# A two-layer decoder trunk: token-major residual and down projections by seven products of halves

## The chip, the cores and the metric

The kernel runs on one core of a Trainium2 chip. The metric is the device time of one execution in microseconds (us); lower is better. The time before is 1746.85 us, the median of three runs (1746.84 to 1747.02).

## The reference

There are 512 tokens of 1024 channels in float32 and two layers. Each layer is

```
x = x + 1/2 * (silu(h @ w1) * (h @ w3)) @ w2      h = rmsnorm(x, g1), 2816 hidden channels
h = rmsnorm(x, gm);  p = h @ w_in                 2048 columns, eight pieces of 256
y = concat(conformer_conv, short_gated_conv, multiscale_pool, chunked_spatial_gating)
x = x + y @ w_out
x = x + 1/2 * swiglu(rmsnorm(x, g2))              as the first line, with its own weights
```

and the output is `rmsnorm(x, final_norm)`. The four mixers are causal over the tokens; the conformer part is a depthwise convolution of 31 taps with a layer norm, a sigmoid gate before it and a silu behind it. `rmsnorm` divides by the root of a token's mean square over the 1024 channels and multiplies by a gain.

## The kernel before

All activations are channel-major: a tile holds 128 channels on the partitions and the 512 tokens along the row. The residual is eight such tiles, `xt[0..7]`.

Each matrix product keeps float32 accuracy with three fast products. A float32 operand is split into a rounded part, `hi`, and a remainder, `lo`. For weights, ScalarE makes `hi` (L92, a copy with a change of type) and VectorE makes `lo = raw - hi` (L94); the same is done for activations. `mm3` (L97) then issues hi\*hi, hi\*lo and lo\*hi into one PSUM bank. Weights arrive by DMA on SyncE's queue in pieces of 128x1024 (512 KB), with four buffers each for the raw piece, for `hi` and for `lo`.

The work on TensorE is written out by hand (`manual_schedule`); the other engines' instructions are ordered by the framework's scheduler, by priority. The stages are: up projections of the first feed-forward part (22 hidden tiles, each with two products of 8 x 3 matmuls of 512 columns); its down projection (8 output tiles, each 22 x 3 matmuls); the mixers (14 projections, the gating values, the output projection); the second feed-forward part; and again for layer two. The trace names the feed-forward parts f0a, f0b, f1a and f1b, and the mixers L0 and L1.

The norm is put off. `Norm.gained` splits gain times x, not yet divided by the root. `Norm.square` sums the squares as the residual's tiles get ready. A few 1-column matmuls (`pst`, L120) sum over channels; GpSimd takes the power -1/2 (L112); four transposes (`pr`, L131) spread the result over the partitions. What was put off is made up by multiplications behind the products (L179 in `up`, `half` in `down`, and L343, L346, L391, L434, L446, L452 in the mixers). So TensorE goes from one stage into the next without waiting for the norm.

In `up` the hidden activation is `a = sigmoid(h1) * h1 * p3` with three VectorE operations (L179, L182, L183), and is split once for all its uses. At the start the first weight tile is loaded in quarters beside the eight residual tiles, so that TensorE starts on the first quarter; ten warming products (`pd`, L199) stand ahead. At the end the last output tile is done in two halves of the tokens, with the final norm of the first half under the second.

Of the kernel before, what the change touches and what calls it, by code (L numbers as in the profile page):

```python
# [12 lines left out]
I32 = mybir.dt.int32  # L13
# [3 lines left out]
P = 128  # L17
T = 512
# [3 lines left out]
KF = DFF // P  # L22
DEPTH = 2
# [3 lines left out]
WARM = 10  # L27
OUT_ORDER = (0, 1, 6, 2, 3, 7, 4, 5)

# columns of the packed per-partition parameters, for each layer  # L30
C_N1, C_NM, C_N2 = 0, 8, 16
C_CW = 24
# [6 lines left out]
C_FN = DEPTH * C_LAYER  # L39
C_IW = C_FN + 8  # L40
# [3 lines left out]
# the three tables of a layer, 512 columns each: gmlp gain and bias; spatial  # L44
# weights (s, h, t); spatial bias and pool weights (block diagonal)
# [3 lines left out]
def trunk(ctx: ExitStack, tc: tile.TileContext, x, par, tab, w13, w2, wi, wg, wo, woa, out):  # L49
# [6 lines left out]
    tmp = ctx.enter_context(tc.tile_pool(name="tmp", bufs=3))  # L56
    small = ctx.enter_context(tc.tile_pool(name="small", bufs=2))
    psm = ctx.enter_context(tc.tile_pool(name="psm", bufs=6, space=bass.MemoryType.PSUM))
    psx = ctx.enter_context(tc.tile_pool(name="psx", bufs=2, space=bass.MemoryType.PSUM))
# [4 lines left out]
    V.memset(ones, 1.0)  # L64
    warm = const.tile([P, 4], F32, name="warm")
    S.activation(warm, ones, AF.Sigmoid)
    gain = const.tile([P, KD], F32, name="gain")
    nc.sync.dma_start(gain, par[:, C_N1 : C_N1 + KD])

    # the residual and the first tile's weights, in the order of their use  # L70
    xt = [acts.tile([P, T], F32, name=f"x{k}", tag=f"x{k}") for k in range(KD)]
    first = [acts.tile([P, 2, 256], F32, name=f"wf{i}", tag=f"s{16 + i}h") for i in range(4)]
    for k in range(KD):
        nc.sync.dma_start(xt[k], x[k])
        if k % 2 == 0:
            c = slice(k * P, (k + 2) * P)
            nc.sync.dma_start(first[k // 2], w13[0, 0, :, :, c].rearrange("a p c -> p a c"))

    pt = const.tile([P, C_ALL], F32, name="pt")
    nc.sync.dma_start(pt, par)  # L80
# [3 lines left out]
    expo = const.tile([P, NB], F32, name="expo")  # L84
    V.memset(expo, -0.5)

# [1 line left out]
    def load_w(src, ncol, name):  # L88
        raw = wts.tile([P, ncol], F32, tag="raw", name=f"raw_{name}")
        nc.sync.dma_start(raw, src)  # L90
        hi = wts.tile([P, ncol], F32R, tag="whi", name=f"whi_{name}")
        S.copy(hi, raw)  # L92
        lo = wts.tile([P, ncol], F32R, tag="wlo", name=f"wlo_{name}")
        V.tensor_tensor(lo, raw, hi.bitcast(F32), ALU.subtract)  # L94
        return hi, lo

    def mm3(ps, hi, lo, xh, xl, first, last):  # L97
        PE.matmul(ps, hi, xh, start=first, stop=False)  # L98
        PE.matmul(ps, hi, xl, start=False, stop=False)  # L99
        PE.matmul(ps, lo, xh, start=False, stop=last)  # L100

    def split(t, name, tag):
        hi = acts.tile([P, T], F32R, tag=f"{tag}h", name=f"{name}h")
        S.copy(hi, t)
        lo = acts.tile([P, T], F32R, tag=f"{tag}l", name=f"{name}l")
        V.tensor_tensor(lo, t, hi.bitcast(F32), ALU.subtract)
        return hi, lo

# [7 lines left out]
    def rstd_of(sqs, n, name, b0=0, nb=NB):  # L116
        ps = psx.tile([P, 512], F32, tag="aux", name=f"pst_{name}")
        for b in range(nb):
            for i, sq in enumerate(sqs):
                PE.matmul(  # L120
                    ps[:, b : b + 1], sq[:, (b0 + b) * P : (b0 + b + 1) * P], ones[:, 0:1],
                    start=(i == 0), stop=(i == len(sqs) - 1),
                )
        v = small.tile([P, nb], F32, tag=f"rv{nb}", name=f"rv_{name}")
        V.tensor_scalar(v, ps[:, 0:nb], 1.0 / n, EPS, ALU.mult, ALU.add)
        return rsqrt(v, nb, name)

    def spread(y, name, nb=NB):
        pr = psx.tile([P, T], F32, tag="aux", name=f"pr_{name}")
        for b in range(nb):  # L130
            PE.transpose(pr[:, b * P : (b + 1) * P], y[:, b : b + 1].broadcast_to([P, P]), ident)  # L131
        return pr

    def row(pr, name):
        r = small.tile([P, T], F32, tag="R", name=f"R_{name}", bufs=1)
        S.copy(r, pr)
        return r

# [1 line left out]
    class Norm:  # L140
        def __init__(self, name, gcol):
            self.name, self.gcol, self.acc, self.h, self.l = name, gcol, None, {}, {}

        def gained(self, k):
            nm = f"{self.name}_{k}"
            g = (gain if self.gcol == C_N1 else pt)[:, self.gcol + k : self.gcol + k + 1]
            hi = acts.tile([P, T], F32R, tag=f"gh{k}", name=f"gh_{nm}")
            S.activation(hi, xt[k], AF.Copy, scale=g)
            lo = acts.tile([P, T], F32R, tag=f"gl{k}", name=f"gl_{nm}")
            V.scalar_tensor_tensor(lo, xt[k], g, hi.bitcast(F32), ALU.mult, ALU.subtract)  # L150
            self.h[k], self.l[k] = hi, lo

        def square(self, k):
            sq = tmp.tile([P, T], F32, tag="sq", name=f"sq_{self.name}_{k}", bufs=2)
            S.activation(sq, xt[k], AF.Square)
            if self.acc is not None:
                V.tensor_tensor(sq, self.acc, sq, ALU.add)
            self.acc = sq

        def add(self, k):  # L160
            if self.gcol is not None:
                with tc.high_priority(offset=300):
                    self.gained(k)
            self.square(k)

        def stats(self):
            self.rc = rstd_of([self.acc], D, self.name)

        def finish(self):
            self.R = row(spread(self.rc, self.name), self.name)  # L170

    def ffn(f, nrm, nxt, name, start=False, end=False):
        ah, al = [], []
        held = []
        j0 = 1

        def up(j, p1, p3):
            h1 = tmp.tile([P, T], F32, tag="h1", name=f"h1_{name}{j}")
            V.tensor_tensor(h1, p1, nrm.R, ALU.mult)  # L179
            a = tmp.tile([P, T], F32, tag="a", name=f"a_{name}{j}")  # L180
            S.activation(a, h1, AF.Sigmoid)
            V.tensor_tensor(a, a, h1, ALU.mult)  # L182
            V.tensor_tensor(a, p3, a, ALU.mult)  # L183
            h, l = split(a, f"a_{name}{j}", f"s{j}")
            ah.append(h)
            al.append(l)

        for j in range(KF):
            p1 = psm.tile([P, T], F32, tag="mm", name=f"p1_{name}{j}")
            p3 = psm.tile([P, T], F32, tag="mm", name=f"p3_{name}{j}")  # L190
            if start and j == 0:
                order = ExitStack()
                order.enter_context(
                    tc.manual_schedule(engines={mybir.EngineType.Activation, mybir.EngineType.DVE})
                )
                # TensorE's clock rises with work
                pd = psx.tile([P, T], F32, tag="aux", name="pd")
                for i in range(WARM):
                    PE.matmul(pd[:, 0:P], mean_w, mean_w, start=True, stop=True)  # L199
                for k in range(KD):  # L200
                    nrm.gained(k)
                    if k % 2 == 0:
                        i = k // 2
                        hi = acts.tile([P, 2, 256], F32R, name=f"wfh{i}", tag=f"s{16 + i}l")
                        S.copy(hi, first[i])
                        q, hl = divmod(i, 2)
                        lo = acts.tile([P, 2, 256], F32R, name=f"wfl{i}", tag=f"s{20 + q}{'hl'[hl]}")
                        V.tensor_tensor(lo, first[i], hi.bitcast(F32), ALU.subtract)
                    c = slice((k % 2) * P, (k % 2 + 1) * P)
                    for i, p in enumerate((p1, p3)):  # L210
                        mm3(p, hi[:, i, c], lo[:, i, c], nrm.h[k], nrm.l[k], k == 0, k == KD - 1)
                    if k >= 2:
                        nrm.square(k - 2)
                for k in range(KD - 2, KD):
                    nrm.square(k)
# [433 lines left out]
```

## Time and profile before

| | |
|---|---|
| median of the runs | 1746.85 us |
| span of the profiled execution | 1744.5 us |
| what lies around the span | 2.35 us |
| TensorE busy | 1733.9 us (99%), 7882 matmuls |
| VectorE busy | 877.9 us (50%) |
| ScalarE busy | 533.5 us (31%) |
| GpSimd busy | 22.0 us (1%) |
| bytes moved | 170.70 MB, mean 98 GB/s |

The profiled execution is read by its span, from its first to its last instruction. The median of the runs is 2.35 us longer; that difference is taken as fixed. PE is TensorE's matmuls, PEld its weight loads, DVE is VectorE, ACT is ScalarE, POOL is GpSimd, SP is SyncE. A matmul's printed duration contains its passage through the array, so for the rate one reads the distance of two starts.

### The profile page before, as it was taken

The numbers are of one execution on the slowest core, as the hardware profiler recorded it, in microseconds if no ns is written. First come the engines' busy times: TensorE is split into PE (matmuls) and PEld (weight loads), VectorE is DVE, ScalarE is ACT, GpSimd is POOL, SyncE is SP. The second block draws the span as 40 slices with busy tenths as digits, with TensorE's granted clock in tenths as the row PEclk, the third lists the DMA queues.
The fourth block names the chain that finished last, engine by engine and source line by source line (L and its number), as shares of the span: only waits on it lengthen the run. The fifth ranks groups of instructions, "written<-read, shape, count | busy, mean of one in ns | idle before, by whom it ended". The sixth has DMA issues, their size and how long they took to land.

```text
span 1744.5 us, 19177 instructions
## 1 busy us (share of the span) xinstructions
PE 1733.9 (99%) x7882; PEld 1438.9 (82%) x7882; DVE 877.9 (50%) x1145; ACT 533.5 (31%) x693; POOL 22.0 (1%) x22
## 2 busy tenths in 40 slices
PE   9999999999999999999999999999999999999997
PEld 7888888888788888888888888888888888888887
DVE  6444443459864444434344444433697554444333
ACT  5222222233243222222232222222333432222221
POOL 0000000000000000000000000000000000000000
PEclk9999999999999999999999999999999999999999
DMA  5222223332232222333322322233222322223321
GB/s 208 97 97 97 97 88 100 103 115 79 85 103 97 97 97 97 94 95 93 105 97 97 97 97 94 91 100 117 89 85 91 103 97 97 97 97 91 97 91 48
DMA packets 52022, 170.70 MB, mean 98 GB/s; under 512 B 5728, under 2 KB 8928, under 8 KB 51936
## 3 DMA queue, kind: packets, MB, share of 16 engines
q1 hardware_dynamic: 51936, 169.50, 30.0%
q8 instruction: 61, 1.00, 0.2%
q14 instruction: 25, 0.20, 0.0%
HBM read 167.38 MB, written 2.10 MB: 97 GB/s over the span
## 4 chain that ended last, share of the span: by engine, by line
PE 99%; DVE 0%; ACT 0%; DMA 0%; issue 0%; SPq 0%; POOLq 0%; DVEq 0%; ACTq 0%
PE p_f1b L98 7%; PE p_f1b L100 7%; PE p_f1a L98 7%; PE p_f1b L99 7%; PE p_f0b L100 7%; PE p_f0b L99 7%; PE p_f0b L98 7%; PE p_f1a L100 7%; PE p_f1a L99 7%; PE p_f0a L100 7%; PE p_f0a L98 7%; PE p_f0a L99 7%; PE pi_L L98 3%; PE pi_L L99 3%; PE pi_L L100 3%; PE po_L L98 2%
## 5 line engine op out<-in xcount | busy, mean ns | idle before, releaser
L502 DVE SCALAR_TENSOR_TENSOR cg_L<-cv_L,pt,cg_L 128x503 f32<-128x503 f32 (+26 forms) x120 | 83.5, 726 | 2.3 <-ACT cg_L L500 1.8
L98 PE MATMUL p_f1b<-gh_b,whi_f1bb 128*128 128x512 f32 x176 | 68.6, 390 | 0.0
L98 PE MATMUL p_f1a<-gh_a,whi_f1ab 128*128 128x512 f32 x176 | 68.6, 390 | 0.0
L98 PE MATMUL p_f0b<-gh_b,whi_f0bb 128*128 128x512 f32 x176 | 68.6, 390 | 0.0
L98 PE MATMUL p_f0b<-gh_b,whi_f0ba 128*128 128x512 f32 x176 | 68.6, 390 | 0.0
L98 PE MATMUL p_f1a<-gh_a,whi_f1aa 128*128 128x512 f32 x176 | 68.6, 390 | 0.0
L98 PE MATMUL p_f1b<-gh_b,whi_f1ba 128*128 128x512 f32 x176 | 68.6, 390 | 0.0
L100 PE MATMUL p_f0b<-gh_b,wlo_f0bb 128*128 128x512 f32 x176 | 68.5, 389 | 0.0
L100 PE MATMUL p_f1b<-gh_b,wlo_f1bb 128*128 128x512 f32 x176 | 68.5, 389 | 0.0
L100 PE MATMUL p_f0b<-gh_b,wlo_f0ba 128*128 128x512 f32 x176 | 68.5, 389 | 0.0
L100 PE MATMUL p_f1a<-gh_a,wlo_f1ab 128*128 128x512 f32 x176 | 68.5, 389 | 0.0
L100 PE MATMUL p_f1b<-gh_b,wlo_f1ba 128*128 128x512 f32 x176 | 68.5, 389 | 0.0
L99 PE MATMUL p_f1a<-gl_a,whi_f1aa 128*128 128x512 f32 x176 | 68.5, 389 | 0.0
L100 PE MATMUL p_f1a<-gh_a,wlo_f1aa 128*128 128x512 f32 x176 | 68.5, 389 | 0.0
L99 PE MATMUL p_f0b<-gl_b,whi_f0ba 128*128 128x512 f32 x176 | 68.5, 389 | 0.0
L99 PE MATMUL p_f1b<-gl_b,whi_f1ba 128*128 128x512 f32 x176 | 68.5, 389 | 0.0
L99 PE MATMUL p_f1a<-gl_a,whi_f1ab 128*128 128x512 f32 x176 | 68.5, 389 | 0.0
L99 PE MATMUL p_f0b<-gl_b,whi_f0bb 128*128 128x512 f32 x176 | 68.5, 389 | 0.0
L99 PE MATMUL p_f1b<-gl_b,whi_f1bb 128*128 128x512 f32 x176 | 68.5, 389 | 0.0
L98 PE MATMUL p_f0a<-gh_n,whi_f0ab 128*128 128x512 f32 x168 | 65.5, 390 | 0.0
L98 PE MATMUL p_f0a<-gh_n,whi_f0aa 128*128 128x512 f32 x168 | 65.5, 390 | 0.0
L99 PE MATMUL p_f0a<-gl_n,whi_f0aa 128*128 128x512 f32 x168 | 65.4, 389 | 0.0
(1074 smaller groups left out, 4434.7 us busy)
## 6 DMA issues: line engine op xcount, KB each, us to landing
raw_f0ba<-w SPq DMA_DIRECT2D x22, 512.0 KB, 3.7
raw_f0bb<-w SPq DMA_DIRECT2D x22, 512.0 KB, 3.6
raw_f1aa<-w SPq DMA_DIRECT2D x22, 512.0 KB, 3.7
raw_f1ab<-w SPq DMA_DIRECT2D x22, 512.0 KB, 3.6
raw_f1ba<-w SPq DMA_DIRECT2D x22, 512.0 KB, 3.7
raw_f1bb<-w SPq DMA_DIRECT2D x22, 512.0 KB, 3.6
raw_f0aa<-w SPq DMA_DIRECT2D x21, 512.0 KB, 3.7
raw_f0ab<-w SPq DMA_DIRECT2D x21, 512.0 KB, 3.6
```

The costliest lines, as they stand in the source:

```text
L98: PE.matmul(ps, hi, xh, start=first, stop=False)
L99: PE.matmul(ps, hi, xl, start=False, stop=False)
L100: PE.matmul(ps, lo, xh, start=False, stop=last)
L502: V.scalar_tensor_tensor(acc[:, kk:], v[:, : T - kk], cw, acc[:, kk:], ALU.mult, ALU.add)
```

## The change

The residual becomes token-major: four tiles of 128 tokens by 1024 channels. What needs channels on the partitions (the products that read a norm) is transposed on TensorE.

`Norm` now works by token tile. `square` is one ScalarE activation per half row with a sum as a by-product; `scale` adds EPS, takes the power on GpSimd and multiplies x by the root and by a gain row (VectorE, 1024 columns); `turn` transposes eight 128x128 blocks into two PSUM banks and splits them from there. The multiplications behind the products are gone.

```
def turn(self, b):
    s = slice(b * P, (b + 1) * P)
    for q in range(2):
        ps = bank(f"pt_{self.name}{b}{q}", (P, 4, P))
        for k in range(4):
            PE.transpose(ps[:, k], self.xn[b][:, (4 * q + k) * P : (4 * q + k + 1) * P], ident)
        S.copy(self.hi[q][:, :, s], ps)
        V.tensor_tensor(self.lo[q][:, :, s], ps, self.hi[q][:, :, s].bitcast(F32), ALU.subtract)
```

A stage that reads a norm starts with token tiles 2 and 3 (r = 1, 256 columns) for its first weights, then TensorE turns tiles 0 and 1, and then the same weights are used on those (r = 0). The other products of the stage use all 512 tokens.

```
for r in (1, 0):
    for _, _, _, _, ps, w in heads:          # two hidden tiles, w1 and w3 each
        for e in range(2):
            for k in range(KD):
                mm3(ps[e][:, HALF[r]], w[e][0][:, c], w[e][1][:, c],
                    nrm.h(k)[:, HALF[r]], nrm.l(k)[:, HALF[r]], k == 0, k == KD - 1)
    if r == 1:
        turns()
```

In `up` the activation is `silu` on ScalarE straight from PSUM and one VectorE product; the hidden activations are no longer split there, but three half-size differences are made for each group (`sums`: `t1 = a21 - a22`, `t2 = t1 - a11`, `a21 = a11 - a21`).

`down` makes the product of A (512 tokens x 2816) and B (2816 x 1024), both cut into four quarters, by seven products of quarters in place of eight. A product is 2 token tiles x 11 hidden tiles x 3 matmuls of 512 columns; the activations are now the stationary operand. Weights come in groups of two hidden tiles (128 x 2 x 512). Sums of weight quarters (`tview`, `b12`) and of activations are made on VectorE and split again for each product:

```
for j in J:                                   # first phase: products a, b
    b11 = piece(0, 0, j, "a")
    av, wv = asplit(quarter(0, 0, j), j, "a"), wsplit(b11, j, "a");       product(X, j, av, wv)
    b12 = piece(0, 1, j, "b")
    V.tensor_tensor(tview(j), b11, b12, ALU.add)
    av, wv = asplit(s1[j], j, "b"), wsplit(tview(j), j, "b");             product(Z, j, av, wv)
for t in range(2): add(0, 0, t, X[t], 1); add(1, 1, t, Z[t], 1)
for j in J:                                   # second phase: c, d
    b12, b22 = piece(0, 1, j, "c"), piece(1, 1, j, "d")
    V.tensor_tensor(b12, b12, b22, ALU.add)
    av, wv = asplit(quarter(1, 0, j), j, "c"), wsplit(b12, j, "c");       product(Q, j, av, wv)
    V.tensor_tensor(tview(j), tview(j), b22, ALU.add)
    av, wv = asplit(s2[j], j, "d"), wsplit(tview(j), j, "d");             product(X, j, av, wv, True)
for t in range(2):
    add(1, 1, t, Q[t], -1); add(0, 1, t, X[t], -1); add(1, 0, t, X[t], 1); add(1, 1, t, X[t], -1)
    nxt.square(2 + t, 1)
for j in J:                                   # third phase: e, f
    b21 = piece(1, 0, j, "e")
    av, wv = asplit(quarter(0, 1, j), j, "e"), wsplit(b21, j, "e")
    V.tensor_tensor(s2[j], s2[j], quarter(0, 1, j), ALU.add);             product(W, j, av, wv)
    V.tensor_tensor(tview(j), tview(j), b21, ALU.add)
    av, wv = asplit(quarter(1, 1, j), j, "f"), wsplit(tview(j), j, "f");  product(Q, j, av, wv, True)
for t in range(2): add(1, 0, t, Q[t], 1); nxt.square(2 + t, 0); nxt.scale(2 + t)
for t in range(2): add(0, 0, t, W[t], 1); nxt.square(t, 0)
for j in J:                                   # fourth phase: g
    b22 = piece(1, 1, j, "g")
    av, wv = asplit(s2[j], j, "g"), wsplit(b22, j, "g")
    if j < 4: product(Z, j, av, wv, True)     # groups 4 and 5 are held, and done by token tile
    if j == 3: nxt.turn(2); nxt.turn(3)
```

Then each of the two token tiles gets its held products, its last `add`, `square` and `scale`. `add` is one VectorE operation from PSUM into the residual, half a row at a time. `piece` loads, so that six quarters of the weights are loaded in place of four. There are six groups (five of two hidden tiles, one of one).

The output projection is token-major too (4 token tiles x 2 halves of the columns, as many matmuls as before), with the conformer's channels last. All eight PSUM banks are one pool. The conformer, the pools and the gates read their projections without a multiplication by the root; the gating values of tokens 2 and 3 come first in the mixers. At the start x tiles 2 and 3 and the gain row are loaded first, then x tiles 0 and 1, the parameters, and the weights; there are 40 warming products. At the end the last `scale` writes the output rows, which are stored by one DMA per token tile.

## Rows read from the trace of the kernel before

**Rows 1.** The page: TensorE's share of the span, and the chain that ended last.

```profile
PE 1733.9 (99%) x7882; PEld 1438.9 (82%) x7882; DVE 877.9 (50%) x1145; ACT 533.5 (31%) x693; POOL 22.0 (1%) x22
...
PE 99%; DVE 0%; ACT 0%; DMA 0%; issue 0%; SPq 0%; POOLq 0%; DVEq 0%; ACTq 0%
```

**Rows 2.** Busy time by window: in f0a's down projection, in mixers L0, before its layer norm.

```profile
core 0: us, PE busy (x) PEld busy (x) DVE busy (x) ACT busy (x) POOL busy (x), PEclk, DMA share, GB/s
...
260.00:360.00 100.00, 100.00 (x443) 82.84 (x442) 40.27 (x48) 28.60 (x35) 1.09 (x1) 1.00 0.34 107
...
440.00:450.00 10.00, 10.00 (x44) 7.91 (x43) 10.00 (x16) 3.09 (x4) 0.00 (x0) 1.00 0.26 81
...
468.60:472.40 3.80, 3.80 (x19) 3.13 (x18) 0.55 (x2) 0.84 (x2) 0.00 (x0) 1.00 0.00 0
```

**Rows 3.** Timeline of TensorE: second and last of the 528 matmuls of f0a's down projection.

```profile
248.62 0.39 PE L99 MATMUL p_f0a<-a_f0a0l,whi_f0ac 128*128 128x512 f32 x1
...
367.85 0.39 PE L100 MATMUL p_f0a<-a_f0a21h,wlo_f0ac 128*128 128x512 f32 x1
```

**Rows 4.** The chain in order of time: a norm's 1-column products, its four transposes.

```profile
24.09 0.79 PE pst_n L120 x8
30.49 0.44 PE pr_n L131 x4
```

**Rows 5.** The gating values' lines: first and last of 96 matmuls of 256 columns.

```profile
L362 PE MATMUL pgv_L<-whi_L0g,gh_m x32: 277/283/284, 391.3 to 402.4; 128*128 128x256 f32 x32
...
L364 PE MATMUL pgv_L<-whi_L0g,gl_m x32: 283/283/283, 391.5 to 402.6; 128*128 128x256 f32 x32
```

**Rows 6.** Timeline of VectorE: back-to-back operations of 1024 and of 512 columns, six taps.

```profile
394.42 4.14 DVE L502 SCALAR_TENSOR_TENSOR cg_L<-cv_L,pt,cg_L 128x504 f32<-128x504 f32 x6
...
539.30 1.22 DVE L94 TENSOR_TENSOR wlo_f0ba<-raw_f0ba,whi_f0ba 128x1024 fp32r<-128x1024 f32 x1
540.44 0.69 DVE L106 TENSOR_TENSOR a_f0b1l<-a_f0b,a_f0b1h 128x512 fp32r<-128x512 f32 x1
541.04 0.69 DVE L182 TENSOR_TENSOR a_f0b<-a_f0b,h_f0b 128x512 f32<-128x512 f32 x1
```

**Rows 7.** Groups by line: sums into the residual, ScalarE's copies of weights and from PSUM.

```profile
L547 DVE TENSOR_TENSOR x<-po_L,x 128x512 f32<-128x512 f32 x16 | 10.9, 684 | 1.0 <-PE po_L L100 1.0
...
L92 ACT CAST whi_f0ac<-raw_f0ac 128x1024 fp32r<-128x1024 f32 x16 | 16.9, 1053 | 50.3 <-issue 27.0 <-PE p_f0a L99 23.4
...
L136 ACT COPY R_m<-pr_m 128x512 f32<-128x512 f32 x2 | 1.2, 581 | 0.0
```

**Rows 8.** Windows of the start; the last number is GB/s.

```profile
0.00:4.00 4.00, 2.88 (x13) 2.88 (x14) 0.19 (x3) 1.49 (x2) 0.70 (x6) 1.00 0.38 114
4.00:8.00 4.00, 3.91 (x16) 2.79 (x14) 1.74 (x3) 2.43 (x4) 0.00 (x0) 1.00 0.93 315
8.00:12.00 4.00, 3.72 (x17) 2.96 (x17) 3.62 (x7) 4.00 (x8) 0.00 (x0) 1.00 1.00 356
```

**Rows 9.** Timeline of TensorE at the start: warming products, early matmuls, the 49th matmul.

```profile
1.12 4.64 PE L199 MATMUL pd<-mean_w 128*128 128x128 f32 x20 [1.12 <-DVE expo L85]
...
6.68 0.40 PE L98 MATMUL p_f0a<-gh_n,wfh 128*128 128x512 f32 x1
6.91 0.39 PE L99 MATMUL p_f0a<-gl_n,wfh 128*128 128x512 f32 x1
...
18.47 0.39 PE L98 MATMUL p_f0a<-gh_n,whi_f0aa 128*128 128x512 f32 x1
```

**Rows 10.** Timeline of the end: last matmul, the power on GpSimd, the last scaling.

```profile
1733.66 0.28 PE L100 MATMUL p_f1b<-a_f1b21h,wlo_f1bc 128*128 128x256 f32 x1
...
1736.65 0.70 POOL L112 TENSOR_TENSOR ry_a<-rv_a,expo 128x2 f32<-128x2 f32 x1 [8.09 <-DVE rv_a L125]
...
1738.13 3.22 DVE L289 SCALAR_TENSOR_TENSOR o<-x,pt,pr_a 128x256 f32<-128x256 f32 x8 [1.65 <-PE pr_a L131]
```

**Rows 11.** Windows of the end; the third number from the right is the granted clock.

```profile
1734.00:1736.00 2.00, 0.61 (x6) 0.55 (x5) 0.83 (x2) 0.42 (x1) 0.00 (x0) 1.00 0.33 109
1736.00:1738.00 2.00, 0.88 (x5) 0.48 (x4) 0.16 (x1) 0.00 (x0) 0.70 (x1) 0.61 0.00 0
```

More of the change, by code (lines that the diff above doesn't have):

```diff
@@ L64, in trunk @@
     V.memset(ones, 1.0)
+    expo = const.tile([P, 4], F32, name="expo")
+    V.memset(expo, -0.5)
     warm = const.tile([P, 4], F32, name="warm")
[L66 to L77, printed above, removed]
@@ L92, in load_w @@
         S.copy(hi, raw)
-        lo = wts.tile([P, ncol], F32R, tag="wlo", name=f"wlo_{name}")
+        lo = pool.tile(list(shape), F32R, tag=tags[1], name=f"wlo_{name}")
         V.tensor_tensor(lo, raw, hi.bitcast(F32), ALU.subtract)
         return hi, lo
[L97 to L107, printed above, removed]
+    def load_w(src, ncol, name):
+        return split_w(load(src, (P, ncol), name), (P, ncol), name)
@@ L110, in rsqrt, with mm3 @@
+    def mm3(ps, sh, sl, mh, ml, first, last, more=False):
+        PE.matmul(ps, sh, mh, start=first, stop=False, skip_group_check=more)
+        PE.matmul(ps, sh, ml, start=False, stop=False, skip_group_check=more)
+        PE.matmul(ps, sl, mh, start=False, stop=last, skip_group_check=more)
     def rsqrt(v, n, name):
@@ L128, in spread @@
[L128 to L215, printed above, removed]
-                order.close()
-            else:
-                w1 = load_w(w13[f, j, 0], D, f"{name}a{j}")
-                w3 = load_w(w13[f, j, 1], D, f"{name}b{j}")
-                for w, p in ((w1, p1), (w3, p3)):
@@ new lines, in ffn, with __init__, __call__ @@
+    def ffn(f, nrm, nxt, name, turns, end=False):
+        down(f, *up(f, nrm, turns, name), nxt, name, end)
+    class Scratch:
+        def __init__(self, nm):
+            self.nm = nm
+            self.f32 = [f"S{j}" for j in range(5)] + [f"U{j}" for j in range(5)] + ["ah"] * 6 + ["al"] * 6
+            self.pairs = {F32: ["a13", "a14"], F32R: [f"a0{j}" for j in range(5)] + [f"a1{j}" for j in range(3)]}
+            self.half = {F32: None, F32R: None}
+        def __call__(self, name, dt=F32, shape=(P, T)):
+            if dt == F32 and self.f32:
+                tag = self.f32.pop(0)
+                return acts.tile(list(shape), F32, tag=tag, name=name, bufs=6 if tag in ("ah", "al") else 1)
+            if self.half[dt] is None:
+                pair = acts.tile([P, 2, T], dt, tag=self.pairs[dt].pop(0), name=f"pair_{name}")
+                self.half[dt] = pair[:, 1]
+                flat = pair[:, 0]
+            else:
+                flat = self.half[dt]
+                self.half[dt] = None
+            if len(shape) == 3:
+                flat = flat.rearrange("p (a b) -> p a b", a=shape[1])
+            return flat
@@ L551, in trunk @@
[L551 to L561 removed]
+        wa = []
@@ new lines, in mixers @@
+        for b in (2, 3):
+            nxt.turn(b)
+    ctx.enter_context(tc.manual_schedule(engines={mybir.EngineType.PE}))
+    pd = bank("pd")
+    for i in range(WARM):
+        PE.matmul(pd[:, 0:P], mean_w, mean_w, start=True, stop=True)
+    nrm = Norm("n0", 0)
+    for b in (2, 3):
+        for c in range(2):
+            nrm.square(b, c)
+        nrm.scale(b)
+    for b in (0, 1):
+        nc.sync.dma_start(xt[b], x[b])
+    for b in (0, 1):
+        for c in range(2):
+            nrm.square(b, c)
+        nrm.scale(b)
@@ new lines, in trunk, with turns @@
+    pt = const.tile([P, C_ALL], F32, name="pt")
+    nc.sync.dma_start(pt, par)
+    for b in (2, 3):
+        nrm.turn(b)
+    for l in range(DEPTH):
+        def turns(nrm=nrm):
+            for b in (0, 1):
+                nrm.turn(b)
+        nx = Norm(f"m{l}", 3 * l + 1)
+        ffn(2 * l, nrm, nx, f"f{l}a", turns)
+        nrm = nx
+        def turns(nrm=nrm):
+            for b in (0, 1):
+                nrm.turn(b)
+        nx = Norm(f"b{l}", 3 * l + 2)
+        mixers(l, nrm, nx, turns)
+        nrm = nx
+        def turns(nrm=nrm):
+            for b in (0, 1):
+                nrm.turn(b)
+        nx = Norm(f"a{l + 1}", 3 * l + 3)
+        ffn(2 * l + 1, nrm, nx, f"f{l}b", turns, end=l + 1 == DEPTH)
```

518 lines of the change are left out of this document (310 added, 208 removed).

## The prediction

> **What bounds the kernel now.** I read the page first: TensorE is busy for 99% of the span, and the chain that ended last lies on it for 99% too [rows 1]. So nothing else sets the time in the middle of the program, and matmuls taken away count in full, as long as what replaces them stays hidden. The windows show what it can hide behind: in the old down projection VectorE works for 40 us of 100 and ScalarE for 29, while DMA engines are busy for 0.34 of the time at 107 GB/s; but in the mixers VectorE has no gap at all [rows 2]. Then the timelines gave unit prices.
>
> **Unit prices.** Between the second and the last matmul of a down projection lie 526 steps in 119.23 us: 0.2267 us for 512 columns [rows 3]. With 256 columns 95 steps take 11.3 us: 0.119 us each [rows 5]. A norm's 1-column products hold TensorE for 0.79 us, four transposes for 0.44, so 0.11 each [rows 4]. VectorE back to back starts a 1024-column operation every 1.14 us and a 512-column one every 0.60, and six taps (a scalar and two tensors) take 4.14 us, or 0.68 each [rows 6]. A sum into the residual reads PSUM in 0.684 us [rows 7]; the new `add` is the taps' kind of operation with a PSUM operand, so I take 0.68 (bounds 0.60 and 0.75).
>
> **The parts on TensorE.**
> - Seven products of 66 matmuls replace 528: 66 fewer in each of four down projections, 264 x 0.2267 = -59.8 us.
> - Six norms lose their 1-column products and four transposes: 6 x 1.23 = -7.4.
> - `turn` brings 32 transposes for each of six norms. The first 16 stand before the first matmul and are counted there; 176 x 0.11 = +19.4.
> - Halves of 256 columns: a pair costs 0.238 where one matmul cost 0.2267. There are 96 pairs in each feed-forward part, 48 in each mixer: 480 x 0.011 = +5.3; the old halves of the last tile (66) go, -0.7.
>
> Together -43.2 us. The output projection has as many matmuls as before: nothing.
>
> **The ends.** Before, 48 matmuls were done at 18.47 [rows 9], as if they had run from 7.6 on. After, x tiles 2 and 3 and the gain (1.57 MB) lie ahead of x tiles 0 and 1 and the parameters (1.17 MB), and these ahead of the first weights (0.52 MB). By the rates of the start (0.46 MB by 4 us, 1.72 by 8, 3.14 by 12) [rows 8] the gain lands at 7.5 and the first weight at 12.4. The forty warming products are 80 instructions. The first 20 took 4.64 us, 0.23 each; the others at the transposes' 0.11 end at about 12.4, too. Then 16 transposes and their splits (below) take 3.4 us: the first matmul at about 15.9, +8.3. At the end 10.8 us lay between the last matmul and the end of the span [rows 10]. After: `add` 0.7, square 0.6 (as a copy of 512 columns [rows 7]), power 0.7 [rows 10], a 1024-column scaling 1.3 (a tap's 0.68 and the 0.54 by which 1024 columns cost more than 512, rounded up), small steps and hand-overs 0.7, and the 3.1 us behind the last scaling plus 0.8 for twice the bytes: 8. I take -2.6.
>
> **The turns.** TensorE gives out 16 transposes in 1.76 us. ScalarE copies a bank in 0.58 [rows 7], VectorE subtracts in 0.60. The third copy, the first matmul's last need, ends about 2.35 us after the turn began, the third remainder at 3.05: TensorE waits 1.2 us. A weight copy (1.05) or a weight remainder that is under way adds about 0.25. For six turns of tiles 0 and 1: 6 x 1.45 = 8.7. Behind the mixers the turn of tiles 2 and 3 is bare as well, and follows a norm that is just done: 2 x 2.2 = 4.4. Behind a down projection 18 held matmuls (4.1 us) cover it; I leave 0.5 for three of these, and 1 us a layer for the three weight pieces of the second half of the output projection, which wait for buffers of the first: +3.5. Both bounds: 0, and a doubling.
>
> GpSimd's powers have one column each (0.70 for two), and the chain of tiles 0 and 1 (4 to 5 us) lies under the 96 first halves (11.4 us). The gain rows and the tables go through SyncE's queue ahead of weights; their buffers are long free, so nothing queues behind them. Six quarters of weights (17.3 MB) in 105 us are 165 GB/s, under the 356 seen at the start [rows 8].
>
> **VectorE in the down projection.** This is the doubtful term. By group of two hidden tiles, TensorE takes 24 x 0.2267 = 5.44 us in phases one to three; with 5.5 groups a phase is 29.9 us. VectorE's work:
> - First: two weight remainders and one sum (1.14 each), two activation remainders (0.60): 4.62, 25.4 a phase.
> - Second: a sum more, 5.76: 31.7, and 4 `add` of the phase before: 34.4.
> - Third: 5.22 with the sum of `s2`: 28.7, and 8 `add`: 34.1.
> - Fourth: 1.74, 9.6; 4 `add`, two scalings of 1024 columns (1.3), four remainders of the turn: 17.3, against 15.0 + 1.8 on TensorE.
>
> So VectorE is short by 4.5, 4.2 and 0.5 us behind a first phase with 4.5 to spare. What it can do ahead: with four weight buffers three products are ready beside the one in use (8.2 us of TensorE's time), and the spare 4.5 go into sums and activation remainders that need none of them. That is 12.7 against 9.2. If it all carries over, a stall of 0.5 us is left. If no lead crosses a phase's border, it is 9.2 and another 3.4, since the fourth phase's `add` and scalings come before its light part: 12.6. I take 3.5 a projection, near the lower bound, because the saturated mixers show VectorE without any gap though its work there waits for ScalarE and TensorE as well [rows 2]; 3% lost on some 85 us is 2.6, and 0.9 for the borders. Four times: +14.0. ScalarE has 2 x 1.05 + 2 x 0.58 = 3.3 of each 5.44 us: hidden.
>
> The mixers' taps: VectorE was done with them before the layer norm's product (0.55 us of work in the 3.8 before it) [rows 2], and loses twelve multiplications of 0.60; they start some 4 us later. Nothing.
>
> **Sum.** -43.2 + 8.3 - 2.6 + 8.7 + 4.4 + 3.5 + 14.0 = -6.9 us. The span of 1744.5 becomes 1737.6; with the 2.35 us around it (the profiled execution is that much below the runs' median) 1740.
>
> **Clock.** At the end, where TensorE stood for most of 1734 to 1736, the granted clock of the next 2 us is 0.61, a mean of the two levels, 2.4 and 1.2 GHz [rows 11]. Waits of a turn are shorter and lie between long stretches of matmuls, so I count nothing. The Trainium skill ("TensorE: Matmul & The Clock Gate", "A second HAM failure mode: psum-queue depth-cycling") says that short idle gaps between groups of matmuls can be enough to make the clock swing between its levels. By that rule the rival below would hold; the trace shows the fall, but no such short gap ahead of one.
>
> **Rivals.**
> - *VectorE becomes the bound of the down projection.* It decides from 5.2 us a projection on (3.5 + 6.9/4), where the gain is gone. With no lead carried it is 12.6 each, +36: 1776; half carried, 1758. For it: 113 us of VectorE's work beside 106 of TensorE's. Against: the lead, and the gapless mixers. Chance 0.30, 1747 to 1776.
> - *Everything is covered.* Stalls of 0.5 us, no transition costs, turns at 1.2 us: 12 + 3.5 + 2.5 less, and a start some 3 us earlier: 1718 to 1728. Chance 0.12.
> - *The clock falls at the bare turns.* At the start 5.6 us passed from the first warming product to the first 0.23 us step of a 512-column matmul [rows 9]; at half speed this costs 2.8 us. Eight turns: +22, 1762. Chance 0.08. Against: the shortness of the gaps.
> - My forecast, 1728 to 1747: 0.45. Another 0.05 for mishaps at the ends, either way.
>
> **The numbers.** A difference of 0.2% (3.5 us) is about what can be told from none. Faster, below 1743.4: 0.38 of the forecast, 0.12, 0.02: 0.52. Same: 0.07 of the forecast's upper edge, 0.06 of the first rival's lower: 0.13. Slower: 0.24 + 0.08 + 0.03 = 0.35. The range is 1717 to 1770: the whole forecast, the covered case, the clock and most of the first rival; likeliest's own 1728 to 1747.
>
> **What would show it.** Right: about 462 matmuls a down projection at 0.2267 us; VectorE at 95% or more in its second and third phase; TensorE's waits there on VectorE's remainders adding to some 3.5 us a projection; waits of 1 to 2 us behind each turn; a first matmul at about 16 us. Wrong: TensorE waiting over 5 us a projection, a granted clock below 1 in the middle, or splits that queue behind an `add` which waits for TensorE, so that the lead is lost at each border.

## The result and the profile after

The changed kernel takes 1762.56 us (median of 4 runs, 1762.09 to 1763.12) beside 1746.84 for the kernel before: 1.009 times, with a 95% interval of 1.0076 to 1.0104. It is slower by 0.9%, where faster was forecast; the time is inside the range and above the forecast's own 1728 to 1747. The profiled execution has a span of 1761.0 us, 23.4 above the forecast 1737.6, and its mean granted clock is 0.991 where it was 0.998.

The page of the changed kernel, TensorE's share and the chain, which answer to [rows 1]:

```profile
PE 1716.4 (97%) x8192; PEld 1437.4 (82%) x8192; DVE 1019.8 (58%) x1273; ACT 633.8 (36%) x886; POOL 29.6 (2%) x42
...
PE 76%; DVE 19%; issue 3%; ACT 1%; DMA 1%; POOL 0%; POOLq 0%; DVEq 0%; ACTq 0%
```

TensorE is busy 17.5 us less, but the chain now lies on VectorE for a fifth of the span. The windows of the four phases of f0a's down projection show where (columns as in [rows 2]: length, busy time of PE, weight loads, VectorE, ScalarE, GpSimd, granted clock, DMA share, GB/s):

```profile
265.76:295.70 29.94, 29.94 (x134) 24.79 (x133) 29.11 (x36) 17.35 (x24) 0.98 (x1) 1.00 0.66 220
295.70:325.60 29.90, 29.90 (x134) 24.76 (x132) 29.90 (x37) 17.27 (x24) 0.00 (x0) 1.00 0.50 166
325.60:360.80 35.20, 32.55 (x135) 25.98 (x134) 33.85 (x46) 20.06 (x31) 0.00 (x0) 0.95 0.31 89
360.80:378.40 17.60, 16.57 (x82) 13.64 (x81) 15.16 (x20) 9.78 (x19) 1.41 (x2) 1.00 0.61 189
```

The first two phases are bare: 29.9 us each, as forecast. The third takes 5.3 us more and also loses clock. The timelines of VectorE and of TensorE at its start (start, length, engine, line):

```profile
324.62 1.28 DVE L274 SCALAR_TENSOR_TENSOR x<-pq_f0a,x 128x512 f32<-128x512 f32 x2
325.82 3.67 DVE L274 SCALAR_TENSOR_TENSOR x<-px_f0a,x 128x512 f32<-128x512 f32 x6
...
330.01 1.22 DVE L99 TENSOR_TENSOR wlo_f0af<-tt_f0a,whi_f0af 128x1024 fp32r<-128x1024 f32 x1
```

```profile
328.32 0.39 PE L107 MATMUL pq_f0a<-whi_f0af,ah_f0af 128*128 128x512 f32 x1
331.28 0.57 PE L108 MATMUL pq_f0a<-wlo_f0af,ah_f0af 128*128 128x512 f32 x1 [2.57 <-DVE wlo_f0af L99]
331.65 0.63 PE L109 MATMUL pq_f0a<-whi_f0af,al_f0af 128*128 128x512 f32 x1
332.07 0.63 PE L107 MATMUL pq_f0a<-whi_f0af,ah_f0af 128*128 128x512 f32 x1
332.50 0.63 PE L108 MATMUL pq_f0a<-wlo_f0af,ah_f0af 128*128 128x512 f32 x1
...
335.03 0.39 PE L108 MATMUL pq_f0a<-wlo_f0af,ah_f0af 128*128 128x512 f32 x1
```

Eight `add`s run as one block of 4.8 us ahead of the remainder that the first product of f needs. TensorE waits 2.57 us, and then its steps are 0.43 us apart instead of 0.23 for 3.4 us: the lower of the clock's two levels, in the middle of the program.

The waits of TensorE, summed by what it waited for (total, times, longest), some of each kind:

```profile
PE p_f0b L108 <- DVE gl_b L161: 2.9, 2, 2.3
...
PE pq_f0a L108 <- DVE wlo_f0af L99: 2.6, 1, 2.6
...
PE p_f0b L107 <- ACT gh_b L160: 2.1, 2, 1.8
...
PE p_f0a L109 <- DVE wlo_f0aa L99: 1.7, 1, 1.7
...
PE pz_f0a L108 <- DVE wlo_f0ag L99: 1.0, 1, 1.0
...
PE p_f1a L108 <- DVE gl_a L161: 0.6, 1, 0.6
```

The waits on `wlo_..f` and `wlo_..g` stand in all four projections (2.5 to 2.7 and 1.0), those on `gl_b` and `gh_b` behind both mixers. Behind the first mixer VectorE scales tiles 0 and 1 ahead of the remainders of the turned tiles 2 and 3:

```profile
525.66 1.28 DVE L145 SCALAR_TENSOR_TENSOR xn_b<-x,ry_b,gain 128x1024 f32<-128x1024 f32 x1
...
527.80 1.28 DVE L145 SCALAR_TENSOR_TENSOR xn_b<-x,ry_b,gain 128x1024 f32<-128x1024 f32 x1
529.00 1.88 DVE L161 TENSOR_TENSOR gl_b<-pt_b,gh_b 128x512 fp32r<-128x512 f32 x3
```

The start has the same order (VectorE's scalings of tiles 0 and 1 from 14.22, `gl_n` from 16.62, the first weight remainder at 19.01). TensorE's timeline there, and the granted clock of a window behind it:

```profile
16.77 0.39 PE L107 MATMUL p_f0a<-gh_n,whi_f0aa 128*128 128x256 f32 x1 [1.77 <-ACT whi_f0aa L97]
17.95 0.58 PE L108 MATMUL p_f0a<-gl_n,whi_f0aa 128*128 128x256 f32 x1 [0.80 <-DVE gl_n L161]
20.28 0.58 PE L109 MATMUL p_f0a<-gh_n,wlo_f0aa 128*128 128x256 f32 x1 [1.75 <-DVE wlo_f0aa L99]
20.66 0.41 PE L107 MATMUL p_f0a<-gh_n,whi_f0aa 128*128 128x256 f32 x1
20.87 0.41 PE L108 MATMUL p_f0a<-gl_n,whi_f0aa 128*128 128x256 f32 x1
```

```profile
20.00:24.00 4.00, 3.72 (x17) 3.72 (x18) 3.63 (x4) 0.00 (x0) 0.00 (x0) 0.50 0.59 186
```

The first matmul comes at 16.8 (forecast 15.9; it comes at 15.3 to 16.3 in five kernels below whose start is the same), the third at 20.3, and the clock is at its lower level for 6.8 us from 17.5 on. In all there are seven such stretches before the end: this one of 6.8 us, and one of 3.4 us in each down projection and behind each mixer. The kernel before has none until 1736.4, behind its last product.

**Where the 23.4 us lie.** Start: f0a's down projection begins at 265.8; from [rows 3] and the forecast's terms it was expected at 259.7: +6.0. Down projections: 112.5, 112.4, 112.6 and 110.7 us from the first start to the last, where 461 steps of 0.2267 and, in three of them, 16 transposes make 106.3 and 104.5: 6.2 each instead of 3.5, +11. Mixers' ends: +3.5 each, +7. The tail behind the last matmul: 9.4 instead of 8, +1.4. The remaining -2 is rounding and what was better than forecast (turns of tiles 0 and 1 wait 0.9, not 1.45).

### The profile page after: what moved, and what is told of

Same layout as the page of the kernel before. It is cut to its first block, busy times and chain, and to the rows that moved or that the text cites. A ratio compares the mean times of both kernels' runs of the same rounds, so it can differ in the third digit from the quotient of the medians.

```text
span 1761.0 us, 20404 instructions
## 1 busy us (share of the span) xinstructions
PE 1716.4 (97%) x8192; PEld 1437.4 (82%) x8192; DVE 1019.8 (58%) x1273; ACT 633.8 (36%) x886; POOL 29.6 (2%) x42
## 3 DMA queue, kind: packets, MB, share of 16 engines
q8 instruction: 64, 1.05, 0.2%
## 4 chain that ended last, share of the span: by engine, by line
PE 76%; DVE 19%; issue 3%; ACT 1%; DMA 1%; POOL 0%; POOLq 0%; DVEq 0%; ACTq 0%
PE p_f0b L108 5%; PE p_f1b L108 5%; PE p_f0a L109 5%; PE p_f0a L108 5%; PE p_f0b L109 5%; PE p_f0a L107 5%; PE p_f1b L109 5%; PE p_f1b L107 5%; PE p_f1a L108 5%; PE p_f1a L109 5%; PE p_f0b L107 5%; PE p_f1a L107 5%; DVE x L274 2%; DVE cg_L L581 2%; PE pi_L L108 2%
## 5 line engine op out<-in xcount | busy, mean ns | idle before, releaser
L581 DVE SCALAR_TENSOR_TENSOR cg_L<-cv_L,pt,cg_L 128x507 f32<-128x507 f32 (+26 forms) x120 | 82.9, 729 | 0.7
L108 PE MATMUL p_f0b<-gl_b,whi_f0ba 128*128 128x512 f32 (+1 forms) x192 | 72.2, 376 | 2.9 <-DVE gl_b L161 2.9
L108 PE MATMUL p_f1b<-gl_b,whi_f1ba 128*128 128x512 f32 (+1 forms) x192 | 72.2, 376 | 2.9 <-DVE gl_b L161 2.9
L107 PE MATMUL p_f0a<-gh_n,whi_f0aa 128*128 128x512 f32 (+1 forms) x192 | 72.3, 377 | 2.1 <-ACT whi_f0aa L97 1.8
L107 PE MATMUL p_f1b<-gh_b,whi_f1ba 128*128 128x512 f32 (+1 forms) x192 | 72.2, 376 | 2.1 <-ACT gh_b L160 2.1
L107 PE MATMUL p_f0b<-gh_b,whi_f0ba 128*128 128x512 f32 (+1 forms) x192 | 72.1, 375 | 2.1 <-ACT gh_b L160 2.1
L109 PE MATMUL p_f0a<-gh_n,wlo_f0aa 128*128 128x512 f32 (+1 forms) x192 | 72.3, 377 | 1.7 <-DVE wlo_f0aa L99 1.7
L108 PE MATMUL p_f0a<-gl_n,whi_f0aa 128*128 128x512 f32 (+1 forms) x192 | 72.5, 378 | 1.4 <-DVE gl_n L161 1.4
L109 PE MATMUL p_f1b<-gh_b,wlo_f1ba 128*128 128x512 f32 (+1 forms) x192 | 72.0, 375 | 0.0
L109 PE MATMUL p_f0b<-gh_b,wlo_f0ba 128*128 128x512 f32 (+1 forms) x192 | 72.0, 375 | 0.0
```

The costliest lines, as they stand in the source:

```text
L107: PE.matmul(ps, sh, mh, start=first, stop=False, skip_group_check=more)
L108: PE.matmul(ps, sh, ml, start=False, stop=False, skip_group_check=more)
L109: PE.matmul(ps, sl, mh, start=False, stop=last, skip_group_check=more)
L581: V.scalar_tensor_tensor(acc[:, kk:], v[:, : T - kk], cw, acc[:, kk:], ALU.mult, ALU.add)
```

## The experiments

Three theories, not exclusive. **A, order:** the block of `add`s and the scalings run ahead of the remainder that TensorE needs next. **B, amount:** VectorE has more work in phases 2 to 4 than TensorE has time, so that a wait only moves when the order is changed. **C, clock:** the waits count more than their length, because the clock falls behind them. All kernels were timed beside the kernel before on the same chip (1746.6 to 1746.9); intervals are of the ratio to it.

**Late sums** (only the `add`s of X, three behind the remainders of each of the first two groups of f).

```
-            add(0, 1, t, X[t], -1)
-            add(1, 0, t, X[t], 1)
-            add(1, 1, t, X[t], -1)
...
             product(Q, j, av, wv, True)
+            if j in LATE:
+                t = LATE.index(j)
+                with tc.issue_after(lo_ins[0]):
+                    add(0, 1, t, X[t], -1, True)
```

> One edit: behind the second phase of each down projection the six sums of X into the residual no longer stand in one block with the two of Q; three come behind the first group's remainders of the third phase, three behind the second group's. Theory A (the block of eight sums stands ahead of the remainder that product f waits for, and the 2.6 us of waiting lets the granted clock fall for 3.4 us): the wait at the first matmul of f goes from 2.6 to under 0.5 us, no clock of 0.50 in the third phase, and the time falls by about 4 x (2.6 + 1.7) = 17 us, to some 1745 us. Theory B (VectorE has too much work over the whole phase): the same wait comes back at later products of the third or fourth phase, and the time stays within 4 us of 1762. Theory C (the clock alone): as A, but only through the clock.

1757.88 us, ratio 1.0062 (1.0047 to 1.0077): 4.7 less than the changed kernel, where A gave 17 and B at most 4. The wait of 2.6 fell to 0.8, but f0a's projection still takes 112.7 us (the others 111.7, 111.0 and 109.2):

```profile
295.30:326.60 31.30, 30.34 (x134) 24.75 (x133) 31.30 (x39) 16.99 (x24) 0.00 (x0) 1.00 0.52 168
326.60:360.20 33.60, 31.89 (x133) 24.35 (x132) 33.59 (x46) 20.03 (x30) 0.00 (x0) 1.00 0.32 93
```

VectorE has no gap in 64.9 us, and the waits are now spread over phases 2 to 4, 1.0 + 1.5 + 0.2 + 1.0 = 3.7 us where there were 3.6; the steps around them are longer than 0.2267 and cost another 2.7. So the order by itself mostly moves waits, as B says. No fall of the clock is left in the down projections, but in f0a the longer steps take what that gave back.

**Filled waits** (no wait removed: 20 products of 128 columns with a constant at the start and 16 behind each mixer, into a bank that is started afresh behind them; 11 with zeros ahead of f in each projection).

```
+                for _ in range(11):
+                    PE.matmul(W[1][:, 0:P], zero, mean_w, start=False, stop=False, skip_group_check=True)
```

> Nothing is moved; the long waits of TensorE are filled with small products (128 columns, about 0.22 us each) that change no result: 11 with a stationary tile of zeros into W ahead of product f, 16 ahead of the first half products behind each mixer, 20 ahead of those at the start. Theory C (the waits cost twice, once themselves and once because the granted clock falls behind them): the seven stretches at 0.50 are gone, each down projection is 1.7 us shorter, each stretch from a mixer's end to the half products 1.7, the start 2 to 3: about 12 us less, 1750 us. Theory D (the fall of the clock is only seen, the matmuls behind wait for VectorE anyway): within 4 us of 1762.

1753.16 us, ratio 1.0035 (1.0023 to 1.0047); the mean clock is 0.999 and no stretch at the lower level is left before the end. The third phase of f0a takes 33.6 us instead of 35.2:

```profile
323.00:356.60 33.60, 33.32 (x155) 27.01 (x154) 33.41 (x45) 19.72 (x30) 0.00 (x0) 1.00 0.31 89
```

Work that computes nothing takes 9.4 us off the changed kernel: C. But the time is still above that of the kernel before, so the clock is not the whole of the loss.

**Order of the scalings** (at the start and behind the mixers tiles 0 and 1 are scaled behind the turn's remainders).

```
+        with tc.issue_after(nxt.turned):
+            for b in (0, 1):
+                nxt.scale(b)
```

> One kind of edit: at the start and behind each mixer the scalings (1024 columns, 1.2 us each) of token tiles 0 and 1 are queued on VectorE behind the remainders of the turn of tiles 2 and 3, where they stood ahead of them. Theory A' (TensorE's wait at a bare turn is mostly work that happens to stand ahead of the remainders): the wait behind each mixer falls from 4.1 us to about 1.5, that at the start by about 2.5, no clock of 0.50 behind the mixers: 8 to 13 us less, 1750 to 1755. Rival (the chain from sums to transposes to split sets the wait): under 3 us less.

1753.73 us, ratio 1.0039 (1.0025 to 1.0053), 8.8 off, as expected. The start lost its first wait on `gl_n` and its half clock (f0a's down projection begins at 262.8 instead of 265.8), and behind the mixers the wait on `gl_b` is 0.34 instead of 2.29. The remaining wait of 1.80 on `gh_b` is still followed by a fall, which was not expected, as these windows show: behind the first mixer, then behind the wait of 2.7 us in the third phase of f0a (none) and of f0b:

```profile
525.00:529.00 4.00, 4.00 (x23) 4.00 (x22) 2.97 (x5) 0.00 (x0) 1.06 (x2) 0.57 0.02 4
328.00:332.00 4.00, 3.65 (x16) 3.03 (x17) 4.00 (x6) 0.81 (x2) 0.00 (x0) 1.00 0.00 0
...
836.00:840.00 4.00, 4.00 (x13) 3.13 (x12) 3.67 (x5) 1.03 (x2) 0.00 (x0) 0.58 0.08 14
```

**Eight products** (the seven products undone, all else kept: each quarter of the weights by each half of the activations, no sums; its code replaces the body of the down projection).

```
-            product(X, j, av, wv)
+        for h, j in K:
+            wv = wsplit(piece(h, 0, j, f"a{h}"), j, f"a{h}")
+            for r in (1, 0):
+                group(Y[r], r, h, j, "a", wv)
```

> The scheme of seven products is undone and nothing else: eight products of quarters (528 matmuls), no sums of quarters, token-major as before the edit. First the left columns for all tokens, then the right columns for tiles 2 and 3, then for tiles 0 and 1. Theory A (the seven products gain 59.9 us of matmuls and give back about 6 us a projection; the loss lies in the token-major norm): 1762.6 + 60 - 25 = about 1797 us. Theory B (what the seven products ask of VectorE costs as much as they save): 1770 or less. Without waits in the down projections the clock should fall only at the start and behind the mixers.

1798.29 us, ratio 1.0293 (1.0278 to 1.0309). No wait stands in its down projections (110 us of TensorE in the window 262 to 372, VectorE 66.5). The seven products are thus worth 35.7 us here; from the rows, 59.8 of matmuls less 4 x 6.2 for stalls and clock would be 35.0. The rest of the change costs 51.4 us (1798.3 beside 1746.9): the token-major layout with its transposes, turns and start, and the clock behind them.

**Sums on GpSimd** (the four kinds of sums of weight quarters).

```
-            V.tensor_tensor(tview(j), b11, b12, ALU.add)
+            G.tensor_tensor(tview(j), b11, b12, ALU.add)
```

> The four kinds of sums of weight quarters (24 instructions of 1.13 to 1.2 us in each down projection) run on GpSimd instead of VectorE; the block of eight sums for X still stands ahead of the split of f. Theory B (VectorE has too much work in phases 2 to 4: 27 us go away from each projection): the phases come to 29.9, 29.9, 29.9 and 17.5 us, no wait over 0.5 us is left in them, the granted clock stays at 1 there, and the time falls by some 18 to 25 us, to 1738 to 1745. Theory A (the block alone makes f wait): the wait ahead of f's first matmul stays at 1.5 to 3 us with its fall of the clock; 1752 to 1760. Third case: a sum takes GpSimd more than about 2.7 us (one is needed for each of its 24 places in about 64 us of phases 1 and 2), so that the splits wait for it and the time is above 1770; and if VectorE's own instructions get longer beside GpSimd's, by the factor that their rows then show.

1868.94 us, ratio 1.0701 (1.0682 to 1.0719): the third case. Two timelines, of GpSimd and of VectorE, in the same microseconds:

```profile
302.17 2.35 POOL L296 TENSOR_TENSOR raw_f0ac<-raw_f0ac,raw_f0ad 128x1024 f32<-128x1024 f32 x1 [3.75 <-DMA raw_f0ad<-w]
304.48 3.35 POOL L299 TENSOR_TENSOR tt_f0a<-tt_f0a,raw_f0ad 128x1024 f32<-128x1024 f32 x1
```

```profile
302.42 3.18 DVE L99 TENSOR_TENSOR wlo_f0ad<-tt_f0a,whi_f0ad 128x1024 fp32r<-128x1024 f32 x1
305.63 3.28 DVE L99 TENSOR_TENSOR wlo_f0ac<-raw_f0ac,whi_f0ac 128x1024 fp32r<-128x1024 f32 x1
```

A remainder that takes VectorE 1.22 us by itself takes 3.2 beside a sum on GpSimd. The Trainium skill ("SBUF — State Buffer", "Who interferes with whom") says that a VectorE instruction with two inputs in SBUF contends with a GpSimd instruction that reads SBUF; the rows agree. So this kernel could not tell A from B. With late sums and late scalings as well:

> The sums of weight quarters on GpSimd, the sums for X spread behind the remainders, and the scalings of tiles 0 and 1 queued behind the turned halves at the start and behind the mixers. Theory B: the waits of the down projections are gone as in the kernel with GpSimd's sums alone, and the order takes another 8 to 9 us; 1729 to 1737. If GpSimd's sums are the new bound, the order still takes its 8 to 9 us from whatever that kernel shows.

1848.41 us, ratio 1.0581 (1.0564 to 1.0598), 20.5 less where 8 to 9 were expected of the order; and with the filling products besides:

> All of it: sums of weight quarters on GpSimd, late sums for X, late scalings, and the filling products at the start and behind the mixers. Theory B: 1726 to 1733, below both kernels. If GpSimd's sums are the new bound: above 1755, and worse than the same kernel with the sums on VectorE.

1849.27 us, ratio 1.0581 (1.0556 to 1.0607): filling gives nothing here, and falls of the clock are left in all four projections.

**Order and filling, sums on VectorE** (late sums, late scalings, 8 products at the start and 10 behind each mixer).

> Late sums for X and late scalings, and 8 products of 128 columns with a constant at the start and 10 behind each mixer, none in the down projections. If the falls of the clock and the waits add up as they did singly (late sums -4.7, order -8.8, filling behind the mixers about -4): 1745 to 1749, no stretch at granted clock 0.50 ahead of the end. If filling and order take the same microseconds twice: 1749 to 1752.

1747.98 us, ratio 1.0006 (0.9996 to 1.0016): the changed kernel's loss is undone, 14.6 us, with all the work of the change in it. Its down projections still take 112.1, 111.1, 111.9 and 109.2 us, with no fall of the clock in them.

**Sums by adding DMAs.** GpSimd's queue issues DMAs that add a quarter of the weights from memory to what lies in SBUF, so no engine computes the sums.

```
-            V.tensor_tensor(tview(j), tview(j), b21, ALU.add)
+            G.dma_start(tview(j), w2[f, 1, 0, :, k : k + n], accum_op=ALU.add)
```

First all four kinds, alone and with the three edits of the kernel above:

> The four kinds of sums of weight quarters are made by DMAs that add to what lies in SBUF (issued by GpSimd's queue), so that neither VectorE nor GpSimd computes them; half as many bytes again are read in the down projections. The order of the sums for X and of the scalings is that of the changed kernel. Theory B (VectorE's work, 27 us too much in each projection, sets the pace of phases 2 to 4): with 27 us of VectorE's work gone the second phase has no wait and the wait ahead of f's first matmul falls below 1 us, the phases come to 29.9, 29.9, 30 and 17.5, no clock falls in them; 62 less 34 for what the start, the mixers' ends and the tail cost leaves 1738 to 1745. Theory A (the block of eight sums alone makes f wait): the wait of 1.9 to 2.9 stays with its clock fall; 1752 to 1760. Third case: the adding DMAs land late (more than some 30 us behind their issue) and the splits wait for them; above 1765, with waits released by a DMA in the rows.

> The same with the sums for X late, the scalings late, and the filling products at the start (8) and behind the mixers (10). Theory B: the kernel with sums on VectorE and these three edits took 1748.0, and its down projections 112.9 us each where 107.2 are bare; 4 x 5 us go: 1726 to 1732, faster than both kernels. If the adding DMAs are late, above 1750.

1802.8 us, ratio 1.032 (1.0301 to 1.0338), and 1785.19, ratio 1.022 (1.0204 to 1.0236). One wait of 10.5 to 11.6 us at the start of each projection, for the first sum by DMA, and the lower clock behind it take more than is gained. In the first kernel f still waits 1.46 us in every projection, behind the block of eight `add`s, with 27 us less work on VectorE:

```profile
PE pq_f0a L108 <- DVE wlo_f0af L99: 1.5, 1, 1.5
```

That wait is the block's own, as A says. The second kernel's waits and windows in f0a:

```profile
PE pz_f0a L112 <- ACT whi_f0ab L102: 10.5, 1, 10.5
```

```profile
260.00:290.00 30.00, 19.03 (x71) 14.78 (x70) 12.66 (x15) 9.31 (x11) 8.71 (x10) 0.77 1.02 254
290.00:320.00 30.00, 30.00 (x134) 24.86 (x133) 23.28 (x31) 17.50 (x24) 10.52 (x12) 1.00 1.06 248
320.00:350.00 30.00, 30.00 (x134) 24.83 (x133) 26.12 (x36) 18.74 (x28) 2.60 (x3) 1.00 0.78 200
```

Behind that wait TensorE has no gap: with 20 us less on VectorE in phases 2 and 3 and no block, they are bare. But the DMA engines are full. So the sums of phase 1 went back to VectorE, first with the block of eight, then with late sums (both with late scalings and filling products):

> Adding DMAs for the sums of phases 2 and 3 only (20 us of VectorE's 27), the sum of phase 1 on VectorE as in the changed kernel; late scalings and filling products at the start and behind the mixers; the block of eight sums for X left as it is. Theory B: phases 2 to 4 bare (29.9, 29.9, 17.5), as in the kernel with all sums on DMAs, and the wait of 10.6 us for the first adding DMA of each projection gone: 1783 less 4 x (10.6 + about 3.5 of half clock behind it) = 1724 to 1732. Theory A: the block alone makes f wait 1.9 or more, with a fall of the clock behind some of these waits: 1734 to 1745.

> The same with the sums for X late. Theory B: as the kernel beside it within 1 us (the block of eight fits once VectorE has 20 us less to do), 1724 to 1732. Theory A: 4 x (1.9 + part of 1.7) = 8 to 14 us below the kernel beside it. Either way faster than both kernels, unless the adding DMAs of phase 2 now land late.

1752.66 us, ratio 1.0036 (1.0022 to 1.0049), and 1747.86, ratio 1.0004 (0.9995 to 1.0014): both above what A and B gave. Now the first product of phase 2 waits 2.2 to 3.0 us in the second kernel, for `whi_..c`, whose quarter a DMA has yet to add to; the DMA share is 1.00 to 1.05 from 265.6 to 326. Last, adding DMAs for phase 3 alone, as the one edit to the changed kernel; the same with late sums, late scalings and filling; and that with the running sum of phase 2 by DMA too:

> The changed kernel with one edit: the six sums of phase 3 (b21 onto the running sum, 6.8 us of VectorE) are made by adding DMAs, one load more in six. Theory B (amount of VectorE's work): the 6.8 us cover the 6.2 that each projection lost; no wait over 0.5 us is left in phases 3 and 4 and their clock falls go; -20 to -25 us, 1738 to 1743. Theory A (the block of eight ahead of the split of f): f still waits 1.5 to 2.9 us in each; -4 to -14 us, 1749 to 1758. If DMAs are late again (waits released by a DMA): above 1760.

> The same edit with late sums for X, late scalings and filling products at the start and behind the mixers. The kernel with these three edits alone took 1748.0 with down projections of 112.9 us; Theory B: the 5.7 us above the bare 107.2 go, 4 x 5.7 = 23: 1725 to 1730. Theory A: the late sums already took what the block costs, and the 5.7 us stay: 1743 to 1748. If the DMAs are late: above 1750.

> The same with the second sum of phase 2 (b22 onto the running sum) made by adding DMAs too, the first one (b12 and b22 for c) on VectorE. Theory B with the DMA engines of phases 1 and 2 having room: as the kernel beside it within 2 us, 1725 to 1730. If the 0.5 MB more a group that phase 2 reads are what was late in the kernels with adding DMAs for both its sums: waits of 1 to 3 us in phase 2, 1735 to 1745.

1748.29 us, ratio 1.0012 (1.0003 to 1.0022), between what A and B gave; 1728.37 us, ratio 0.9896 (0.9881 to 0.9911), as B gave; 1758.53 us, ratio 1.0068 (1.0051 to 1.0084), above both cases. The second is faster than both kernels. The wait of f in the first (with the block of eight) and its third phase, and phases 2 to 4 in the second (without the block), all of f0a:

```profile
PE pq_f0a L108 <- DVE wlo_f0af L99: 1.4, 1, 1.4
```

```profile
324.90:356.70 31.80, 30.44 (x134) 24.87 (x133) 28.54 (x40) 18.97 (x29) 0.00 (x0) 1.00 0.40 118
```

```profile
292.26:322.16 29.90, 29.85 (x132) 24.38 (x131) 29.90 (x38) 17.55 (x25) 5.31 (x6) 1.00 0.92 247
322.16:352.10 29.94, 29.94 (x134) 24.79 (x133) 28.65 (x40) 18.71 (x29) 0.00 (x0) 1.00 0.44 129
352.10:369.20 17.10, 17.10 (x86) 14.38 (x84) 15.53 (x21) 10.63 (x20) 1.94 (x2) 1.00 0.60 206
```

With 6.8 us off VectorE and the block in place f waits 1.4 to 1.5 us (2.4 in f1b); without the block the waits are gone, and the four projections take 106.6, 106.3, 106.3 and 105.0 us, bare to 0.5. Beside the kernel with late sums, late scalings and filling, this one edit is worth 19.6 us. Over all four projections the time above the bare 423.3 us is 25 in the changed kernel, 21 without the block alone, 9 without the six sums alone, and 1 without either. B carries most, A the rest. In the third kernel the first product of phase 2 waits 3.9 us again: VectorE stands for the plain load of `raw_f0ad`, at a DMA share of 1.00 in phase 1, and its clock falls:

```profile
PE pq_f0a L113 <- DVE wlo_f0ac L104: 4.2, 2, 3.9
```

## Why the prediction was wrong

Its sum held in the parts on TensorE: bare projections come out at 106.3 to 106.6 and 105.0 us against 106.3 and 104.5 of the working. The kernel with eight products parts the rest. The seven products were to gain 45.8 us (59.8 less 14.0) and gained 35.7; all else was to cost 38.9 and cost 51.4.

**The first step that failed is "I count nothing" for the clock.** The reason given, that waits of a turn are short and lie between long stretches of matmuls, was no protection: waits of 1.8 to 2.7 us were followed by falls. In each of the six stretches of 3.4 us the steps lose up to half of it, 1.7 us; at the start 18 steps of 0.21 us instead of 0.12 lose 1.6, since TensorE stood for part of the 6.8. That is some 12 us that are not in the sum, and filling took 9.4 of them back. A granted clock below 1 in the middle is one of the prediction's own signs of being wrong. It was also the rival at 0.08, though by other prices and at other places: some 12 us rather than 22, and four of the seven stretches stand in the down projections and not at turns. The rule that the prediction quotes from the Trainium skill ("TensorE: Matmul & The Clock Gate", "A second HAM failure mode: psum-queue depth-cycling"), that short idle gaps can be enough, agrees with the trace after.

**VectorE in the down projections** was placed rightly, and its waits add up as forecast: 2.57 + 1.03 = 3.6 us in f0a beside 3.5, with VectorE without a gap in phase 2. That is partly luck: the working had 2.6 of its 3.5 as 3% of 85 us, lost all along, but phase 2 lost nothing, and the time went in two single waits. What failed is the size of the whole term, 6.2 a projection: 1.7 is the clock behind the first wait, and about 0.8 lies in the steps around the waits, which are longer than 0.2267. Also the reason given for a small loss held only in part: the lead is gone by the third phase, whose `add`s come in one block ahead of the split of f. That is nearer to the "wrong" sign of the prediction (splits queued behind `add`s) than to its right one, though these `add`s did not wait for TensorE.

**The bare turns.** For tiles 0 and 1 they were cheaper than forecast, 0.9 against 1.45. Behind the mixers 2.2 was forecast, and 4.1 of waits plus up to 1.7 of clock were measured: the working counted copies and remainders, but not the two scalings of tiles 0 and 1 (1.28 us each) that VectorE runs ahead of them. The same omission made half of the start's 6.0 us, which the order of the scalings took 3.0 off. They lie in 0.9 to the first matmul, 3.5 in the two waits behind it with the steps around them, and 1.6 of clock.

**The rivals.** VectorE as the bound decided from 5.2 us a projection, and 6.2 was measured. Without the clock it is 4.5 by the steps, and 5.0 to 5.6 in the kernel with filled waits, so that rival (0.30, 1747 to 1776) came about, close to its border. The direction was turned by no single term: filling alone left 1753.2 us and the order of the scalings alone 1753.7, both above the kernel before. With late scalings, late sums and filling the time was 1748, no change; the forecast's 1740 needed the waits that B names gone as well, and then 1728 was there.

What stays open: why equal waits are followed by a fall in one place and not in another.

## What to carry to other kernels

When work moves from the engine that bounds a kernel to one beside it, compare the two phase by phase, the sums at each border included: an average of 58% hid a helper that worked 63.8 of 65.1 us in phases 2 and 3. Price a wait of TensorE by what comes behind it as well, since waits of 1.8 to 2.7 us cost up to 1.7 us more here through the clock, and look which ready but unneeded operations the schedule sets ahead of the one that TensorE needs. Where a helper engine has too much to do, neither a second engine on the same memory nor the DMA engines are free: read their own share in the same phase, and move only what fits.

## What the runs showed that was not expected

- The clock falls in the middle of the program, with TensorE busy for 97% of the span. Of four waits of 2.7 to 3.0 us in the third phases of the kernel with late scalings, those in f0b and f1b were followed by a stretch at the lower level, those in f0a and f1a not.
- GpSimd takes 2.3 to 2.9 us on average over a group of sums of weight quarters, VectorE 1.13 to 1.20 over the same groups, and running both makes a VectorE remainder up to 3.4 us long.
- An adding DMA uses the DMA engines 1.9 times as long for a byte as a plain load does: in the window 260 to 367 of the fastest kernel 2.88 MB held 15.5% of them, 17.50 MB of plain loads 49.3%. One of 512 KB landed 6.7 us after its issue there, and 8.9 and 11.7 (two kinds) where both sums of phase 2 were made so, against 3.5 to 5.5 and 3.5 to 8.4 for plain loads.
